# A decoder layer on one core: where three merged activation quads live, and how early weight pairs are begun at a stage border

## The chip, the cores and the metric

The kernel runs on one core of one Trainium2 chip. The metric is the device time of one execution in microseconds (us); a change is judged by the median of several executions. Four engines do the work here: TensorE (PE) multiplies matrices and writes to PSUM banks, VectorE (DVE) and ScalarE (ACT) do elementwise work, GpSimd (POOL) mostly issues DMAs here, and SyncE (SP) issues the weight loads. Each engine works through its own instructions in order; between engines there are semaphore waits.

## The reference

One layer on 256 tokens of width 2048, all in float32. The projection goes to three attention branches of eight heads each and to three gates; each branch result is projected, multiplied by its gate and added up; the sum is projected again. A SwiGLU sub-layer with a hidden width of 5632 and a final norm follow.

```python
def hybrid_mixer(h, w_in, b_gate, ..., w_branch, w_out, lambda_init):
    proj = h @ w_in
    qa, ka, va, qb, kb, vb, qc, kc, vc, g = jnp.split(proj, COL_OFFSETS, axis=-1)
    ...
    br = jnp.stack([_merge_heads(o_a), _merge_heads(o_b), _merge_heads(o_c)], axis=2)
    z = jnp.einsum('bsnm,nmd->bsnd', br, w_branch)
    gates = jax.nn.sigmoid((g + b_gate).reshape(b, s, N_BRANCH, D_MODEL))
    merged = jnp.sum(gates * z, axis=2)
    return merged @ w_out

def swiglu(h, w_gate, w_up, w_down):
    return (jax.nn.silu(h @ w_gate) * (h @ w_up)) @ w_down

x = x + hybrid_mixer(rms_norm(x, norm_mix_g), ...)
x = x + swiglu(rms_norm(x, norm_ffn_g), w_ffn_gate, w_ffn_up, w_ffn_down)
return rms_norm(x, final_norm_g)
```

## The kernel before

**Precision.** A float32 operand is split in two float32r parts, high and low, and a product is three matmuls: high by high, high by low, low by high. An activation is kept transposed as a *quad*: a high and a low part of 512 rows by 256 tokens (128 partitions, 4 by 256 each). A weight block of 512 by 512 is loaded whole (one MB, `raw`), and split on the way: ACT copies the high part, DVE subtracts to get the low part (lines 819 and 820 for half a block, `wboth`; lines 805 and 810 for a whole block in the feed-forward, `wh` and `wl`).

**Units and stages.** The work is a list of *units*, each with a `prep` (split a weight) and an `emit` (its matmuls). In the mixing stage a unit is half a raw block on both token halves, 12 matmuls, lines 799 to 801. There are 18 jobs of eight units for q, k and v, with attention run as side work between units. Then for each of four column blocks j come three gate jobs of eight units and three branch jobs of four, and then four output jobs of eight. The feed-forward has eleven jobs of eleven units each, in a form that replaces eight block products by seven (`m_unit`, on combinations `sp` of the activations and sums of weights) for half of the depth, and multiplies the other half plainly (`p_unit`, 24 matmuls). Its matmuls are lines 789, 790 and 793. The down projection ends the list.

**Memory.** There are two pools on the chip. `bigs` has 17 buffers of 8 KB a partition: raw weights, splits, and quads made by `new_both`. `slots` has 15 of 4 KB: everything small, and quads made by `new_quad`, one slot for each part. A tile waits until the last reader of the buffer's previous tile has ended. Stages limit themselves: three raws in the mixing stage and six in the feed-forward (`RAWS`), four parts of prepared splits in the one and nine in the other (`PARTS`).

**Merged quads.** When the third branch of column block j has been added in (`evac_z`, lines 456 and 461), `to_quad` transposes the merged block on PE and writes its quad, ("m", j). The output jobs read the four of them in their order: units 1 and 2 of a job read m(0), units 3 and 4 m(1), and so on.

**Side work.** One step of a queue of generators is taken per unit (`advance(1)`), ahead of that unit's matmuls. After an output job its `go` adds x, transposes it, and writes `ht` (first two jobs) or a quad `hq` (last two, lines 541 and 542). After the second, `combine` makes four sums in two slots (`s12`, `s34`) and seven `sp` tiles, one slot each, one a step. After a feed-forward job, `f_out` transposes its result and stores it by a POOL DMA.

**Order.** Instructions stand on each engine in the order of the program. The main loop prepares ahead and then emits:

```python
    for u, (need, later, stage, _, emit) in enumerate(units):
        prepare_units(u + 4 if stage == "mix" else u + 6)
        advance(1)
        todo, deferred[:] = deferred[:], []
        emit(ready.popleft())
```

`prepare_units` begins units while parts are free. A feed-forward unit is prepared as a pair: `high` when it is begun and `low` a step later, so the two stand at different places in the queues. An `m_unit` adds other raws into its own first (line 611) and then lets POOL add the next weight into a raw by an accumulating DMA (line 621).

Of the kernel before, what the change touches and what calls it, by code (L numbers as in the profile page):

```python
# [27 lines left out]
AF = mybir.ActivationFunctionType  # L28
# [3 lines left out]
P = 128  # L32
# [19 lines left out]
def trunk(ctx, tc, xT, x, gmix, gffn, w_in, b_gate, lq1, lk1, lq2, lk2, subln, w_branch, w_out,  # L52
          w_fg, w_fu, w_fd, gfin, out):
    nc = tc.nc
# [10 lines left out]
    def slot(shape, name, dt=F32):  # L65
        return slots.tile(shape, dt, tag="slot", name=name)

    def big(shape, name, dt=F32):

        return bigs.tile(shape, dt, tag="big", name=name)  # L70
# [78 lines left out]
    def advance(n):  # L149
        while n > 0 and side:  # L150
            try:
                next(side[0])
                n -= 1
            except StopIteration:
                side.popleft()
# [9 lines left out]
    def new_quad(name):  # L165
        return slot([P, 4, S], name + "h", F32R), slot([P, 4, S], name + "l", F32R)

    def new_both():

        t = big([P, 2, 4, S], "hq", F32R)  # L170
        return t[:, 0], t[:, 1]
# [32 lines left out]
    def transposes(dst, srcs):  # L204
        for i, s in enumerate(srcs):
            nc.tensor.transpose(dst[:, i * P:(i + 1) * P], s, ident)  # L206

    def tps():
        return side_ps.tile([P, 512], F32, tag="T", name="tps")
# [4 lines left out]
    def to_parts(ps, h, l):  # L214
        nc.scalar.activation(h, ps, AF.Copy)
        nc.vector.tensor_tensor(l, ps, h.bitcast(F32), OP.subtract)

    def to_quad(key, nat):

        yield  # L220
        h, l = new_both()
        for t in range(2):
            ps = tps()
            transposes(ps, [nat[:, t, i * P:(i + 1) * P] for i in range(4)])
            to_parts(ps.rearrange("p (a b) -> p a b", a=4), h[:, :, t * P:(t + 1) * P],
                     l[:, :, t * P:(t + 1) * P])
            if t == 1:
                quads[key] = (h, l)
            yield
# [222 lines left out]
    def evac_z(n, j):  # L452
        def f(pss):
            s = sig.pop((n, j))
            for t in range(2):
                nc.vector.tensor_tensor(s[:, t], pss[t], s[:, t], OP.mult)  # L456
            if n == 0:
                merged[j] = s
            else:
                m = merged[j]  # L460
                nc.vector.tensor_tensor(m, m, s, OP.add)
                if n == 2:
                    side.append(to_quad(("m", j), m))
        return f
# [101 lines left out]
    f_t = [scratch.tile([P, 4, S], F32, name=f"f_t{j}") for j in range(NCF)]  # L566

    def f_out(j, f):

        yield  # L570
        ft = slot([P, 4, S], "ft")
        for t in range(2):
            ps = tps()
            transposes(ps, [f[:, t, i * P:(i + 1) * P] for i in range(4)])
            nc.scalar.activation(ft[:, :, t * P:(t + 1) * P], ps.rearrange("p (a b) -> p a b", a=4), AF.Copy)
            if t == 1:
                nc.gpsimd.dma_start(f_t[j], ft)
            yield

    f_in = {}  # L580

# [14 lines left out]
    def ffn_job(j):  # L596
# [80 lines left out]
        def up():  # L677

            s = v["s"]
            nc.vector.tensor_tensor(s[:, 1], bank["b6"], s[:, 1], OP.mult)  # L680
            nc.vector.tensor_tensor(v["m1"], bank["b1"], v["m1"], OP.add)
            nc.vector.tensor_tensor(s[:, 0], v["m1"], s[:, 0], OP.mult)
            side.append(f_out(j, s))
# [71 lines left out]
    units = []  # L755
# [175 lines left out]
    at = 0  # L931

    def prepare_units(n):


        nonlocal at, held

        def low_part():
            nonlocal held
            need, gen = begun.popleft()  # L940
            ready.append(next(gen))
            held += need

        while at < len(units) and at < n:
            need, later, stage, prep, _ = units[at]
            room = PARTS[stage] - held
            if len(begun) > 1 and begun[0][0] <= room:
                low_part()
                continue
            if need > room or len(begun) > 1:  # L950
                break
            gen = prep()
            next(gen)
            begun.append((later, gen))
            held += need
            at += 1
            if not later:
                while begun:
                    low_part()
        while begun and (at == len(units) or not ready):  # L960
            low_part()

    prepare_units(3)
    side.append(prepare())
    for u, (need, later, stage, _, emit) in enumerate(units):
        prepare_units(u + 4 if stage == "mix" else u + 6)
        advance(1)
        todo, deferred[:] = deferred[:], []
        emit(ready.popleft())
        held -= need + later  # L970
        for f in todo:
            f()
# [46 lines left out]
```

## Time and profile before

| | |
|---|---|
| median of three executions | 1731.98 us (1722.41 to 1737.12) |
| the profiled execution | 1732.95 us |
| span of its trace | 1730.8 us |
| mean granted PE clock | 0.984 |
| busy: PE, DVE, ACT, POOL | 1675.8, 1065.6, 825.5, 59.4 us |
| HBM read | 343.56 MB |

Lines of a profile name an engine, a source line, an operation and the tiles, written and read; in a timeline the first number is the start from the span's beginning and the second the duration, both in us, and in brackets stands the idle time before, with what ended it. Matmuls are pipelined: a matmul of 128x512 is shown with 0.39 us, while the next one starts after 0.23.

### The profile page before, as it was taken

The numbers are of one execution on the slowest core, as the hardware profiler recorded it, in microseconds if no ns is written. First come the engines' busy times: TensorE is split into PE (matmuls) and PEld (weight loads), VectorE is DVE, ScalarE is ACT, GpSimd is POOL, SyncE is SP. The second block draws the span as 40 slices with busy tenths as digits, with TensorE's granted clock in tenths as the row PEclk, the third lists the DMA queues.
The fourth block names the chain that finished last, engine by engine and source line by source line (L and its number), as shares of the span: only waits on it lengthen the run. The fifth ranks groups of instructions, "written<-read, shape, count | busy, mean of one in ns | idle before, by whom it ended". The sixth has DMA issues, their size and how long they took to land.

```text
span 1730.8 us, 18729 instructions
## 1 busy us (share of the span) xinstructions
PE 1675.8 (97%) x7512; PEld 1369.8 (79%) x7512; DVE 1065.6 (62%) x1077; ACT 825.5 (48%) x950; POOL 59.4 (3%) x87
## 2 busy tenths in 40 slices
PE   9999999999999999986799989999999999999997
PEld 6888888888888887874578868888888888888886
DVE  6676655555655455542155668877778887654563
ACT  7354544444444443432153556655656566443442
POOL 2100000000000000000000000000000001100000
PEclk9999999999999999998799989999999999999999
DMA  9544444454555555542266657888888888755561
GB/s 336 178 170 152 165 169 160 159 176 158 173 204 201 183 194 194 207 153 93 94 219 231 232 157 229 277 270 270 272 261 262 270 268 260 276 176 193 193 238 76
DMA packets 53656, 352.65 MB, mean 204 GB/s; under 512 B 6256, under 2 KB 6528, under 8 KB 13760
## 3 DMA queue, kind: packets, MB, share of 16 engines
q1 hardware_dynamic: 44640, 309.35, 49.4%
q0 software_dynamic: 8208, 41.04, 10.2%
q8 instruction: 59, 0.97, 0.2%
q10 hardware_dynamic: 720, 1.06, 0.2%
q14 instruction: 29, 0.24, 0.0%
HBM read 343.56 MB, written 7.86 MB: 203 GB/s over the span
## 4 chain that ended last, share of the span: by engine, by line
PE 94%; DVE 3%; ACT 2%; DMA 1%; issue 0%; SPq 0%; ACTq 0%
PE acc L800 22%; PE acc L801 22%; PE acc L799 21%; PE acc L789 9%; PE acc L790 8%; PE acc L793 8%; PE tps L206 2%; DVE wboth L820 1%; ACT wboth L819 1%; PE sps L245 1%; DMA raw<-w_in_t 1%; DVE wl L810 1%; DVE raw L611 0%; ACT wh L805 0%; DVE sig L456 0%
## 5 line engine op out<-in xcount | busy, mean ns | idle before, releaser
L820 DVE TENSOR_TENSOR wboth<-raw,wboth 128x1024 fp32r<-128x1024 f32 (+1 forms) x410 | 500.6, 1234 | 379.6 <-ACT wboth L819 379.2
L799 PE MATMUL acc<-wboth,hq 128*128 128x512 f32 x1568 | 632.4, 403 | 17.1 <-ACT wboth L819 17.0
L800 PE MATMUL acc<-wboth,hq 128*128 128x512 f32 x1568 | 620.3, 396 | 12.4 <-DVE wboth L820 12.4
L819 ACT ACTIVATE wboth<-raw 128x1024 fp32r<-128x1024 f32 (+1 forms) x410 | 423.7, 1052 | 413.6 <-PE acc L801 355.9
L801 PE MATMUL acc<-wboth,hq 128*128 128x512 f32 x1568 | 619.6, 395 | 0.0
L799 PEld LDWEIGHTS acc<-wboth,hq 128*128 128x128 f32 x1568 | 299.0, 191 | 86.7 <-ACT wboth L819 25.2
L800 PEld LDWEIGHTS acc<-wboth,hq 128*128 128x128 f32 x1568 | 299.1, 191 | 78.1 <-DVE wboth L820 18.5
L801 PEld LDWEIGHTS acc<-wboth,hq 128*128 128x128 f32 x1568 | 298.7, 190 | 64.2
L810 DVE TENSOR_TENSOR wl<-raw,wh 128x2048 fp32r<-128x2048 f32 x121 | 276.0, 2289 | 81.6 <-PE acc L793 46.5
L805 ACT ACTIVATE wh<-raw 128x2048 fp32r<-128x2048 f32 x121 | 229.0, 1912 | 111.9 <-DVE raw L611 51.0
L789 PE MATMUL acc<-wh,hq 128*128 128x512 f32 x352 | 139.1, 395 | 4.5 <-ACT m L662 4.5
L790 PE MATMUL acc<-wh,hq 128*128 128x512 f32 x352 | 137.9, 392 | 0.0
L789 PE MATMUL acc<-wh,sp 128*128 128x512 f32 x308 | 121.8, 395 | 0.0
L790 PE MATMUL acc<-wh,sp 128*128 128x512 f32 x308 | 120.7, 392 | 0.0
L793 PE MATMUL acc<-wl,hq 128*128 128x512 f32 x352 | 94.5, 390 | 0.0
L793 PE MATMUL acc<-wl,sp 128*128 128x512 f32 x308 | 82.7, 390 | 3.5 <-DVE wl L810 3.5
L789 PEld LDWEIGHTS acc<-wh,hq 128*128 128x128 f32 x352 | 66.6, 189 | 18.5 <-ACT m L662 4.9
L793 PEld LDWEIGHTS acc<-wl,hq 128*128 128x128 f32 x352 | 66.5, 189 | 13.9
L790 PEld LDWEIGHTS acc<-wh,hq 128*128 128x128 f32 x352 | 66.7, 189 | 13.5
L793 PEld LDWEIGHTS acc<-wl,sp 128*128 128x128 f32 x308 | 57.7, 188 | 16.1 <-DVE wl L810 3.9
L789 PEld LDWEIGHTS acc<-wh,sp 128*128 128x128 f32 x308 | 58.4, 190 | 11.8
L790 PEld LDWEIGHTS acc<-wh,sp 128*128 128x128 f32 x308 | 58.3, 189 | 11.9
(185 smaller groups left out, 882.8 us busy)
## 6 DMA issues: line engine op xcount, KB each, us to landing
raw<-w_in_t SPq DMA_DIRECT2D x116, 1024.0 KB, 4.9
raw<-w_fu_t SPq DMA_DIRECT2D x44, 1024.0 KB, 5.0
raw<-w_fg_t SPq DMA_DIRECT2D x44, 1024.0 KB, 6.5
raw<-w_fd_t SPq DMA_DIRECT2D x44, 1024.0 KB, 4.9
raw<-w_branch_t SPq DMA_DIRECT2D x24, 1024.0 KB, 4.9
raw<-w_out_t SPq DMA_DIRECT2D x16, 1024.0 KB, 4.9
raw<-w_fg_t POOLq DMA_DIRECT2D x11, 1024.0 KB, 8.0
raw<-w_fu_t POOLq DMA_DIRECT2D x11, 1024.0 KB, 9.2
```

What stands on the lines that cost most here:

```text
L206: nc.tensor.transpose(dst[:, i * P:(i + 1) * P], s, ident)
L245: nc.tensor.matmul(ps[:, a:b], qt[lo:hi, h, t * P:(t + 1) * P], kt[lo:hi, h, 0:b - a], start=True, stop=True)
L789: nc.tensor.matmul(acc, ah[:, k], wh[:, k], start=first, stop=False, skip_group_check=not start)
L790: nc.tensor.matmul(acc, al[:, k], wh[:, k], start=False, stop=False, skip_group_check=not start)
L793: nc.tensor.matmul(acc, ah[:, k], wl[:, k], start=False, stop=k == 3, skip_group_check=not start)
L799: nc.tensor.matmul(acc, ah[:, k], wh[:, k], start=start and k == 0, stop=False)
L800: nc.tensor.matmul(acc, ah[:, k], wl[:, k], start=False, stop=False)
L801: nc.tensor.matmul(acc, al[:, k], wh[:, k], start=False, stop=stop and k == n - 1)
L805: nc.scalar.activation(h, r, AF.Copy)
L810: nc.vector.tensor_tensor(l, r, h.bitcast(F32), OP.subtract)
L819: nc.scalar.activation(h[:, sl], r[:, sl], AF.Copy)
L820: nc.vector.tensor_tensor(l[:, sl], r[:, sl], h[:, sl].bitcast(F32), OP.subtract)
```

## The change

Three things change. The quads of the first three column blocks are made by `new_quad` (two slots each) rather than `new_both` (one big buffer); the fourth stays. How far ahead a unit may be begun goes by its own stage rather than by the stage of the unit now running: four ahead, and six for a feed-forward unit. And `f_out` makes both of its transpose sets in one step and both copies in the next.

```diff
@@ to_quad
-        h, l = new_both()
+        h, l = new_quad("m") if key[1] < 3 else new_both()
@@ f_out
         yield
+        ps = [tps() for _ in range(2)]
+        for t in range(2):
+            transposes(ps[t], [f[:, t, i * P:(i + 1) * P] for i in range(4)])
+        yield
         ft = slot([P, 4, S], "ft")
         for t in range(2):
-            ps = tps()
-            transposes(ps, [f[:, t, i * P:(i + 1) * P] for i in range(4)])
-            nc.scalar.activation(ft[:, :, t * P:(t + 1) * P], ps.rearrange("p (a b) -> p a b", a=4), AF.Copy)
-            if t == 1:
-                nc.gpsimd.dma_start(f_t[j], ft)
-            yield
+            nc.scalar.activation(ft[:, :, t * P:(t + 1) * P], ps[t].rearrange("p (a b) -> p a b", a=4), AF.Copy)
+        nc.gpsimd.dma_start(f_t[j], ft)
+        yield
@@ prepare_units
-        while at < len(units) and at < n:
+        while at < len(units):
             need, later, stage, prep, _ = units[at]
+            if at >= n + (2 if stage == "ffn" else 0):
+                break
@@ the main loop
-        prepare_units(u + 4 if stage == "mix" else u + 6)
+        prepare_units(u + 4)
```

Up to the border of the two stages every engine keeps its order, and only the buffers differ. Lines behind `f_out` have numbers one higher in the changed kernel (line 820 is 819 before, 821 is 820, 806 is 805, 811 is 810).

On ACT at the end of the fourth output job, from the sixth of the `sp` tiles on, before (the seven `sp` are interleaved with splits, here for that job's units 6 to 8; `wh` are high parts for the feed-forward; the `hq` rows read the transposed x of the third job):

```order
L511 ACTIVATE sp_6609<-s12_6480 128x512
L819 ACTIVATE wboth_6624<-raw_6501 128x1024
L511 ACTIVATE sp_6629<-s34_6481 128x512
L819 ACTIVATE wboth_6644<-raw_6539 128x1024
L819 ACTIVATE wboth_6659<-raw_6539 128x1024
L805 ACTIVATE wh_6676<-raw_6541 128x2048
L805 ACTIVATE wh_6690<-raw_6543 128x2048
L541 ACTIVATE hq_6692<-tps_6693,gf_99 128x256 x2
L805 ACTIVATE wh_6717<-raw_6541 128x2048
L541 ACTIVATE hq_6692<-tps_6719,gf_99 128x256 x2
L805 ACTIVATE wh_6744<-raw_6585 128x2048
```

And now, at the same place:

```order
L511 ACTIVATE sp_6612<-s12_6483 128x512
L820 ACTIVATE wboth_6627<-raw_6504 128x1024
L511 ACTIVATE sp_6632<-s34_6484 128x512
L820 ACTIVATE wboth_6647<-raw_6542 128x1024
L820 ACTIVATE wboth_6662<-raw_6542 128x1024
L806 ACTIVATE wh_6667<-raw_6544 128x2048
L806 ACTIVATE wh_6669<-raw_6546 128x2048
L806 ACTIVATE wh_6686<-raw_6544 128x2048
L806 ACTIVATE wh_6702<-raw_6588 128x2048
L541 ACTIVATE hq_6704<-tps_6705,gf_99 128x256 x2
L806 ACTIVATE wh_6730<-raw_6544 128x2048
L541 ACTIVATE hq_6704<-tps_6732,gf_99 128x256 x2
```

Four high parts stand ahead of the first copies of x where two stood.

On DVE at the same place, before, behind the last split low part of the fourth job (`wl` are low parts, line 611 adds raws, line 522 adds the fourth job's result to x and so frees its banks):

```order
L820 TENSOR_TENSOR wboth_6659<-raw_6539,wboth_6659 128x1024
L542 SCALAR_TENSOR_TENSOR hq_6692<-tps_6693,gf_99,hq_6692 128x256 x2
L810 TENSOR_TENSOR wl_6714<-raw_6541,wh_6676 128x2048
L611 TENSOR_TENSOR raw_6541<-raw_6541,raw_6545 128x2048
L542 SCALAR_TENSOR_TENSOR hq_6692<-tps_6719,gf_99,hq_6692 128x256 x2
L522 TENSOR_TENSOR x2_6590<-acc0_6592,x2_6590 128x512
L522 TENSOR_TENSOR x2_6590<-acc1_6593,x2_6590 128x512
L810 TENSOR_TENSOR wl_6742<-raw_6543,wh_6690 128x2048
```

And now:

```order
L821 TENSOR_TENSOR wboth_6662<-raw_6542,wboth_6662 128x1024
L811 TENSOR_TENSOR wl_6683<-raw_6544,wh_6667 128x2048
L612 TENSOR_TENSOR raw_6544<-raw_6544,raw_6548 128x2048
L811 TENSOR_TENSOR wl_6700<-raw_6546,wh_6669 128x2048
L542 SCALAR_TENSOR_TENSOR hq_6704<-tps_6705,gf_99,hq_6704 128x256 x2
L811 TENSOR_TENSOR wl_6726<-raw_6544,wh_6686 128x2048
L612 TENSOR_TENSOR raw_6544<-raw_6544,raw_6546 128x2048
L542 SCALAR_TENSOR_TENSOR hq_6704<-tps_6732,gf_99,hq_6704 128x256 x2
L522 TENSOR_TENSOR x2_6593<-acc0_6595,x2_6593 128x512
L522 TENSOR_TENSOR x2_6593<-acc1_6596,x2_6593 128x512
```

Ahead of the two additions of line 522 now stand three low parts and two additions of raws, where one of each stood.

On ACT in the second feed-forward job, before (`ft` is the copy of the transposed result, `m` and `u` are copies that free a bank):

```order
L662 ACTIVATE m_7076<-acc_7063 128x512
L805 ACTIVATE wh_7082<-raw_6939 128x2048
L805 ACTIVATE wh_7102<-raw_6869 128x2048
L575 ACTIVATE ft_7108<-tps_7109 128x4x128
L662 ACTIVATE m_7076<-acc_7115 128x512
L805 ACTIVATE wh_7129<-raw_6962 128x2048
L575 ACTIVATE ft_7108<-tps_7135 128x4x128
L805 ACTIVATE wh_7166<-raw_7061 128x2048
L662 ACTIVATE u_7077<-acc_7063 128x512
```

And now:

```order
L663 ACTIVATE m_7079<-acc_7066 128x512
L806 ACTIVATE wh_7085<-raw_6942 128x2048
L806 ACTIVATE wh_7105<-raw_6872 128x2048
L663 ACTIVATE m_7079<-acc_7121 128x512
L806 ACTIVATE wh_7135<-raw_6965 128x2048
L577 ACTIVATE ft_7141<-tps_7111 128x4x128
L577 ACTIVATE ft_7141<-tps_7112 128x4x128
L806 ACTIVATE wh_7169<-raw_7064 128x2048
L663 ACTIVATE u_7080<-acc_7066 128x512
```

Both copies now stand together, behind the second `m` and ahead of the `u`.

## The prediction

> **What bounds the kernel now.** I read the page's slices first, then windows over the thin ones, then PE's waits, then the timeline inside them. A unit is below one weight split of 512 or 256 rows with the matmuls on it (12 of 128x512; a pair of token halves in the feed-forward, "p", has 24).
>
> ```profile
> span 1730.8 us, 18729 instructions
> PE   9999999999999999986799989999999999999997
> PEclk9999999999999999998799989999999999999999
> ```
>
> PE is full except in slices 18 to 20 and in slice 24. The windows (us, PE busy and count, PEld, DVE, ACT, POOL, clock, DMA share, GB/s) show their size:
>
> ```profile
> 692.00:752.00 60.00, 60.00 (x266) 49.71 (x265) 30.96 (x29) 25.43 (x25) 0.08 (x1) 1.00 0.58 202
> 752.00:872.00 120.00, 88.08 (x275) 62.52 (x275) 35.86 (x35) 26.25 (x26) 0.00 (x0) 0.83 0.28 97
> 872.00:1002.00 130.00, 130.00 (x587) 107.62 (x586) 75.73 (x77) 63.46 (x76) 0.72 (x1) 1.00 0.64 230
> 1002.00:1036.00 34.00, 26.06 (x106) 20.66 (x105) 25.02 (x19) 17.75 (x21) 1.80 (x2) 0.85 0.65 168
> 1036.00:1100.00 64.00, 64.00 (x289) 53.02 (x288) 52.99 (x42) 40.76 (x35) 3.17 (x4) 1.00 0.76 248
> ```
>
> Count matmuls, not busy time: 752 to 872 has 275 in 120 us, the stretch before it 266 in 60. PE's waits are few and all there:
>
> ```profile
> PE acc L799 <- ACT wboth L819: 17.0, 15, 1.1
> PE acc L800 <- DVE wboth L820: 12.4, 19, 0.8
> PE tps L206 <- DVE sig L461: 7.2, 2, 5.0
> ```
>
> One unit of the thin stretch, from the timeline (start, duration, engine, line):
>
> ```profile
> 831.24 0.40 PE L801 MATMUL acc<-wboth,hq 128*128 128x512 f32 x1
> 831.67 1.06 ACT L819 ACTIVATE wboth<-raw 128x1024 fp32r<-128x1024 f32 x1 [5.73 <-PE acc L801]
> 832.76 1.23 DVE L820 TENSOR_TENSOR wboth<-raw,wboth 128x1024 fp32r<-128x1024 f32 x1 [5.57 <-ACT wboth L819]
> 832.78 0.51 PE L799 MATMUL acc<-wboth,hq 128*128 128x512 f32 x1 [1.15 <-ACT wboth L819]
> 834.04 0.77 PE L800 MATMUL acc<-wboth,hq 128*128 128x512 f32 x1 [0.76 <-DVE wboth L820]
> 834.61 0.63 PE L801 MATMUL acc<-wboth,hq 128*128 128x512 f32 x1
> 838.46 1.06 ACT L819 ACTIVATE wboth<-raw 128x1024 fp32r<-128x1024 f32 x1 [5.73 <-PE acc L801]
> ```
>
> ACT may write the next split only when PE has read the last one: a single split buffer, strictly serial, 838.46 - 831.67 = 6.79 us a unit. That follows from the code. Of 17 big buffers four hold h, six the branch outputs, three the raw weights; the merged quads m(0), m(1), m(2) take one each as column blocks are finished, so four buffers for splits become three, two and, from the last block's gates on, one.
>
> **Term 1, the merged quads in slots.** m(0) to m(2) leave the big pool, so all gates keep four split buffers. What the full rate is worth there:
>
> ```profile
> 664.49 0.63 PE L206 MATMUL tps<-ident,sig 128*128 128x128 f32 x4 [2.24 <-DVE sig L461]
> 769.16 1.04 PE L206 MATMUL tps<-ident,sig 128*128 128x128 f32 x4 [4.96 <-DVE sig L461]
> 1002.87 0.60 PE L206 MATMUL tps<-ident,x 128*128 128x128 f32 x4
> 1003.23 0.48 PE L799 MATMUL acc<-wboth,hq 128*128 128x512 f32 x1
> 1037.98 0.91 PE acc L793 x4
> 1040.70 0.91 PE acc L793 x4
> ```
>
> A unit at full rate takes 1040.70 - 1037.98 = 2.72 us (the last two rows, from the chain), a group of four transposes 1003.23 - 1002.87 = 0.36. The group at 769.16 (m(2)) stands ahead of the last block's second unit, the one at 1002.87 ahead of the seventh unit of the fourth output job: 35 + 24 + 6 = 65 units and 8 groups, 65 x 2.72 + 8 x 0.36 = 179.7 us. They took 233.7: 54.0 lost. The waits ahead of the m(2) and m(1) groups (4.96, 2.24) are the same shortage: the merging L456/L461 stand on DVE behind a split low part that waits for a buffer; ahead of m(0)'s group, with four buffers, there is no such wait. Sum 61.2. Bounds: with two buffers 692 to 752 ran at full rate, so four should lose nothing; were half of the 54.0 kept by something else, the term would be 34.2. I take 61.2. Raw weights are no limit by the rows: one MB in 5.44 us is 193 GB/s, and 202 flowed at 692.
>
> **Term 2, the border to the feed-forward.** Here both the slots and the earlier start act, against each other. The durations and the old waits:
>
> ```profile
> 985.00 0.61 ACT L511 ACTIVATE sp<-s 128x512 fp32r<-128x512 f32 x1
> 987.36 1.22 DVE L820 TENSOR_TENSOR wboth<-raw,wboth 128x1024 fp32r<-128x1024 f32 x1
> 988.49 0.69 DVE L512 TENSOR_TENSOR sp<-s,sp 128x512 fp32r<-128x512 f32 x1
> 1003.51 0.48 ACT L541 ACTIVATE hq<-tps,gf 128x256 fp32r<-128x256 f32 x1 [4.88 <-PE tps L206]
> 1004.02 0.48 DVE L542 SCALAR_TENSOR_TENSOR hq<-tps,gf,hq 128x256 fp32r<-128x256 f32 x1 [9.10 <-ACT hq L541]
> 1005.44 2.28 DVE L810 TENSOR_TENSOR wl<-raw,wh 128x2048 fp32r<-128x2048 f32 x1
> 1007.76 2.29 DVE L611 TENSOR_TENSOR raw<-raw 128x2048 f32<-128x2048 f32 x1
> 1010.15 1.92 ACT L805 ACTIVATE wh<-raw 128x2048 fp32r<-128x2048 f32 x1 [5.14 <-DVE raw L611]
> 1013.89 1.28 DVE L522 TENSOR_TENSOR x<-acc,x 128x512 f32<-128x512 f32 x2
> 1017.41 1.28 PE L793 MATMUL acc<-wl,sp 128*128 128x512 f32 x4 [3.46 <-DVE wl L810]
> 1021.88 0.40 PE L789 MATMUL acc<-wh,sp 128*128 128x512 f32 x1
> 1026.59 0.88 POOL L621 DMA_DIRECT2D raw<-w_fu_t  x1 [14.97 <-DVE wl L810]
> 1030.47 0.59 ACT L662 ACTIVATE m<-acc 128x512 f32<-128x512 f32 x1
> 1031.12 0.80 PE L789 MATMUL acc<-wh,hq 128*128 128x512 f32 x1 [4.49 <-ACT m L662]
> 1035.99 0.40 PE L789 MATMUL acc<-wh,sp 128*128 128x512 f32 x1
> ```
>
> Call the fourth output job's units o1 to o8 and the feed-forward's f1 to f5 (m0, m2, m4, p, m5). From the transposes ahead of o7 (1002.87) to f5 (1035.99) went 33.1 us; full rate is 7 x 2.72 + 4 x 0.36 = 20.5. So 12.6 are lost: DVE's low part for f2 is late (3.46), then ACT's copy of a bank for f4 (4.49), the rest is slow clock (1017.41 to 1021.88 after the first, and again after the second).
>
> Now slots: at the combining step 15 must hold 6 halves of m, 3 blocks of x, 2 ht, 2 sums: 13. The first two sp fit, the third takes a freed ht, the fourth and fifth must wait for m(0)'s halves, read last by o2, the last two for m(1)'s, read last by o4. These waits stand on ACT ahead of the splits for o4 and after. Counted from T0, the end of o2 (1002.87 - 4 x 2.72 = 991.99 in this trace): sp on ACT 0.2 to 0.8, the split for o4 to 1.75; DVE has sp 0.69, two L522 1.28, then o4's low part, done at 3.9. PE wants it at 2.95: 1.0 lost. The next pair costs 0.15 at o6. ACT ends o8's split at 10.75 (before: it began wh for f1 at T0 + 2.9). Then, in the new order, wh f1, f2 to 14.4; DVE wl f1 14.9, add 17.1, wl f2 19.4; ACT wh f3 19.05, wh f4 20.9; only then the L541/L542 pair (1003.51 to 1005.44, 1.95) to 22.85; wl f3 25.1, second add 27.3; ACT wh f5 29.25; the other pair 31.2; and only then the two L522 of the fourth job, 32.4. PE reaches the transposes of that x, ahead of f3, at 23.6 and needs those L522: a wait of 8.9. Slow clock for 4.5 us as after the 3.46: f3 ends at 37.7, f4's first bank at 40.7, its second waits for ACT's copy to 40.75 and ends at 43.5. Before, f5 began at T0 + 44.0. **Term 2 is -0.5**: the earlier pairs are eaten by the later start of ACT and by L522's place behind three low parts and two additions. POOL's two accumulating loads move with the additions and low parts ahead of them; the second, issued behind f5's low part, goes out at T0 + 36.9 where it went at 34.6 (1026.59), and its raw is next split for f10, which starts past T0 + 60. SP's loads keep their order. Bounds: nothing lost at all, -12.6; three more handoffs of the sort at 1003.51, +6.
>
> The Trainium skill, "TensorE: Matmul & The Clock Gate", section "HAM oscillation — how this bites in real kernels", holds that only gaps over some 3.4 us bring the clock down. By it the 1.0 at o4 costs only itself. The trace differs: gaps of 1.15 and 0.76 at 832 are followed by matmuls of 0.63, and from 834.04 eleven at full rate would have ended 1.7 earlier. By that row o4 would cost 1.7 more; but the transposes at 664.49, after 2.24 idle, are followed by full rate, which is nearer (one gap, not a train), so I add nothing.
>
> **Term 3, f_out.** Same eight transposes and two copies a job, both copies now behind m5's bank copy and ahead of u2's.
>
> ```profile
> ACT u L662 <- PE acc L793: 41.7, 22, 4.0
> ```
>
> ACT waits 41.7/22 = 1.9 us for PE ahead of such a copy, one more 0.6 copy fits; PE is full from 1036 on, so there is nothing to gain either. Zero, covered by that slack; without the cover 11 x 0.6 = 6.6. The store of f is issued in the same unit as before. In the down stage the new limit of four is the one that its four parts set already: zero.
>
> **Sum.** The profiled execution took 1732.95 (2.15 around its span); less 61.2, less 0.5: 1671.2. The median shown is 0.97 lower: **1670**.
>
> **Rivals.** *The border runs clean* (18 in 100): ACT's 4.88 and DVE's 9.10 of waiting before 1004 are filled, and L522 comes in time. Then 12 more go: 1658. Against: L522's place in DVE's order. *Half of term 1 stays* (14 in 100), because raw weights or evacuations bind once splits do not: 1732 - 34 = 1698, or 1685 if a quarter stays. Against: 202 GB/s at full PE in 692 to 752. *Slower* (2 in 100): in each of eleven feed-forward jobs u2's bank copy, now behind both copies of f, is late for m6, as m5's was at 1031.12. A wait of 4.49 and its slow clock (some 2.1) are 6.6, eleven times 72.6: 1743. It decides from 61.7/11 = 5.6 us a job; the slack of 1.9 speaks against. *The change does not act* (2 in 100): the slots' waits serialize what the big pool did; but from T0 to f5 there are only 11 units, at 4.07 lost each 45 us: 1716 at most with term 1 intact, 1732 only if raws also bind.
>
> **Numbers.** Forecast, 64 in 100: 1662 to 1677 (the two terms right to a few us, and a median of runs that lay from 1722.41 to 1737.12). The range reaches to the clean border and a quarter of term 1: 1658 to 1683. A measurement here can tell about 1% from no change: faster by more 0.95, within 0.03, slower 0.02.
>
> **What would show it.** 752 to 810 in the new trace at 266 matmuls per 60 us, no ACT wait on L801 followed by a PE wait on the split; the transposes ahead of f3 waiting about 9 us for L522; a PE wait near 1 us on the low part of o4. Wrong, if PE waits in the gates for raw weights, if the border's wait is under 3 or over 14, or if PE shows gaps once a job after the border.

## The result and the profile after

| | before | changed |
|---|---|---|
| median | 1732.08 us | 1670.86 us |
| lowest to highest, 4 runs each | 1722.41 to 1737.12 | 1670.27 to 1671.43 |
| the profiled execution | 1732.95 us | 1671.43 us |
| span of its trace | 1730.8 us | 1669.3 us |
| mean granted PE clock | 0.984 | 0.996 |

The ratio is 0.9653, with a 95% interval of 0.9611 to 0.9695: faster by 3.5%, 61 us, where 1670.0 had been forecast. The page of the changed kernel first, its span and the slices of PE and of PE's clock:

```profile
span 1669.3 us, 18730 instructions
PE   9999999999999999999999899999999999999997
PEclk9999999999999999999999989999999999999999
```

The thin slices 18 to 20 are gone. Slices are now 41.7 us long; the one that is left, number 23, with the clock low in number 24, is the border (930 to 975 us). The windows say it in matmuls (us, PE busy and count, PEld, DVE, ACT, POOL, clock, DMA share, GB/s):

```profile
692.00:752.00 60.00, 60.00 (x266) 49.70 (x265) 32.84 (x32) 25.25 (x24) 0.71 (x1) 1.00 0.55 192
752.00:812.00 60.00, 60.00 (x270) 49.66 (x269) 33.21 (x32) 26.55 (x27) 1.43 (x2) 1.00 0.66 231
812.00:872.00 60.00, 60.00 (x270) 49.68 (x269) 37.93 (x37) 27.60 (x29) 0.00 (x0) 1.00 0.68 240
955.00:975.00 20.00, 12.68 (x47) 10.17 (x48) 15.72 (x15) 13.20 (x17) 0.88 (x1) 0.74 0.69 206
1040.00:1600.00 560.00, 560.00 (x2511) 464.34 (x2510) 396.10 (x264) 304.25 (x257) 26.66 (x39) 1.00 0.76 248
```

From 752 to 872 there were 275 matmuls in 120 us; now there are 538 (two of the 270 and 270 stand in both windows). DMA carries 231 to 240 GB/s there where it carried 97. From 1040 to 1600 PE has no gap. PE's longest waits (us in total, times, longest):

```profile
PE tps L206 <- DVE x L522: 7.8, 1, 7.8
PE acc L801 <- DVE wboth L821: 1.8, 4, 0.8
PE wps L86 <- DVE ones L81: 1.3, 1, 1.3
PE acc L800 <- ACT wboth L820: 0.6, 2, 0.4
```

The waits for splits (17.0 and 12.4) and for the merging (7.2) have become 2.4 in all. At the border a single new wait of 7.8 stands where there were two, of 3.5 and 4.5. (The wait of 1.3 lies at the start of the execution, in both kernels.) The timeline of the changed kernel there, with the two merging groups ahead of it (start, duration, engine, line; idle time before and its releaser in brackets):

```profile
662.00 0.60 PE L206 MATMUL tps<-ident,sig 128*128 128x128 f32 x4
760.88 0.60 PE L206 MATMUL tps<-ident,sig 128*128 128x128 f32 x4
930.58 0.63 ACT L511 ACTIVATE sp<-ht 128x512 fp32r<-128x512 f32 x1 [12.63 <-PE acc L801]
934.32 0.50 PE L801 MATMUL acc<-wboth,mh 128*128 128x512 f32 x1 [0.61 <-DVE wboth L821]
934.66 0.40 PE L802 MATMUL acc<-wboth,ml 128*128 128x512 f32 x1
936.92 0.63 ACT L511 ACTIVATE sp<-s 128x512 fp32r<-128x512 f32 x1 [3.29 <-PE acc L801]
940.82 3.71 ACT L806 ACTIVATE wh<-raw 128x2048 fp32r<-128x2048 f32 x2
942.45 0.60 PE L206 MATMUL tps<-ident,x 128*128 128x128 f32 x4
961.46 1.28 DVE L522 TENSOR_TENSOR x<-acc,x 128x512 f32<-128x512 f32 x2
962.20 1.50 PE L206 MATMUL tps<-ident,x 128*128 128x128 f32 x4 [7.76 <-DVE x L522]
963.92 0.63 PE L791 MATMUL acc<-wh,sp 128*128 128x512 f32 x1
968.50 0.60 PE L206 MATMUL tps<-ident,x 128*128 128x128 f32 x4
970.14 0.59 ACT L663 ACTIVATE m<-acc 128x512 f32<-128x512 f32 x1
974.44 0.39 PE L790 MATMUL acc<-wh,sp 128*128 128x512 f32 x1
```

The two rows of ACT's L511 are the waits for slots: 930.58 is the moment at which o2 ends (T0, 930.6), and 936.92 that at which o4 ends. Everything that ACT does for the feed-forward stands behind them; its first `wh` begins at 940.82, T0 + 10.2. The row at 962.20 is the new wait of PE ahead of f3, and 974.44 is the start of f5.

So the 61.5 us between the two spans split as follows. The m(1) group comes at 662.00 instead of 664.49, and the m(2) group at 760.88 instead of 769.16: 8.3 us by then. From the m(2) group to o7's transposes it takes 942.45 - 760.88 = 181.6 instead of 1002.87 - 769.16 = 233.7: 52.1. From there to f5 974.44 - 942.45 = 32.0 instead of 33.1: 1.1. The sum is 61.5.

### The profile page after: what moved, and what is told of

Read it like the earlier page. It is cut to its first block, busy times and chain, and to the rows that moved or that the text cites. A ratio compares the mean times of both kernels' runs of the same rounds, so it can differ in the third digit from the quotient of the medians.

```text
span 1669.3 us, 18730 instructions
## 1 busy us (share of the span) xinstructions
PE 1648.2 (99%) x7512; PEld 1357.8 (81%) x7512; DVE 1065.6 (64%) x1077; ACT 824.3 (49%) x950; POOL 60.0 (4%) x87
## 4 chain that ended last, share of the span: by engine, by line
PE 97%; DVE 1%; ACT 1%; DMA 1%; issue 0%; SPq 0%; ACTq 0%; DVEq 0%
PE acc L800 22%; PE acc L802 22%; PE acc L801 22%; PE acc L790 9%; PE acc L791 9%; PE acc L794 9%; PE tps L206 2%; PE sps L245 1%; DMA raw<-w_in_t 1%; ACT wh L806 0%; DVE raw L612 0%; DVE wl L811 0%; ACT wboth L820 0%; PE sps L258 0%; PE sps L259 0%
## 5 line engine op out<-in xcount | busy, mean ns | idle before, releaser
L800 PE MATMUL acc<-wboth,hq 128*128 128x512 f32 x1472 | 586.5, 398 | 0.7 <-ACT wboth L820 0.6
L801 PE MATMUL acc<-wboth,hq 128*128 128x512 f32 x1472 | 573.4, 390 | 1.2 <-DVE wboth L821 1.2
L802 PE MATMUL acc<-wboth,hq 128*128 128x512 f32 x1472 | 574.5, 390 | 0.0
L802 PEld LDWEIGHTS acc<-wboth,hq 128*128 128x128 f32 x1472 | 276.2, 188 | 59.7
L800 PEld LDWEIGHTS acc<-wboth,hq 128*128 128x128 f32 x1472 | 276.5, 188 | 58.8 <-issue 2.7
L801 PEld LDWEIGHTS acc<-wboth,hq 128*128 128x128 f32 x1472 | 276.8, 188 | 57.3 <-DVE wboth L821 2.5
L794 PEld LDWEIGHTS acc<-wl,sp 128*128 128x128 f32 x308 | 58.4, 190 | 12.4
```

The source lines that it names most:

```text
L794: nc.tensor.matmul(acc, ah[:, k], wl[:, k], start=False, stop=k == 3, skip_group_check=not start)
L800: nc.tensor.matmul(acc, ah[:, k], wh[:, k], start=start and k == 0, stop=False)
L801: nc.tensor.matmul(acc, ah[:, k], wl[:, k], start=False, stop=False)
L802: nc.tensor.matmul(acc, al[:, k], wh[:, k], start=False, stop=stop and k == n - 1)
```

## The experiments

One theory stood behind all of them: nearly all of the gain is the four split buffers in the gates; at the border the early start of the feed-forward pairs is worth several us, but the seven `sp`, which now wait on ACT for slots, give them back. Its rivals were that the earlier start alone matters at the border, that the order of DVE (L522 behind three low parts) is what costs there, and that `f_out` counts. Runs of one batch share the runs of the kernel before: the first four have 1731.89 us (13 runs, 1724.49 to 1737.85), the last three 1733.85 (6 runs, 1724.12 to 1737.80).

The measure for the border is the stretch from the transposes ahead of o7 to the first matmul of f5, 33.1 us before and 32.0 in the changed kernel; at full rate it would be 20.5. The wait at o4 lies ahead of it.

### The slots alone

```diff
 (kernel before)
-        h, l = new_both()
+        h, l = new_quad("m") if key[1] < 3 else new_both()
```

> The kernel before with the first three merged quads in slots, nothing else. By the theory of the prediction term 1 comes whole and the border keeps the old order but gets the slots' waits: DVE has the first hq pair ahead of the first low part, f2's low part comes about 5 us late and f4's second bank again waits for ACT's copy; f5 begins about 46 us after the end of o2 (43.8 in the changed kernel), so 1673 us. Rival, that the earlier pairs carry a large part of the gain: over 1680.

Measured: 1674.20 us (1673.37 to 1674.87), ratio 0.9654 (0.9635 to 0.9673). From the timeline of this run, o7's transposes, the two waits of PE and f5:

```profile
943.01 0.60 PE L206 MATMUL tps<-ident,x 128*128 128x128 f32 x4
958.89 2.07 PE L793 MATMUL acc<-wl,sp 128*128 128x512 f32 x4 [4.80 <-DVE wl L810]
972.65 0.79 PE L789 MATMUL acc<-wh,hq 128*128 128x512 f32 x1 [4.65 <-ACT m L662]
976.99 0.39 PE L789 MATMUL acc<-wh,sp 128*128 128x512 f32 x1
```

The line of `to_quad` alone brings 57.7 of the 61 us. The stretch from o7 to f5 is 976.99 - 943.01 = 34.0, with the two waits of before still there (3.46 has become 4.80, 4.49 is 4.65). That is 0.9 more than before, and about 1.0 is lost at o4 besides, where the trace shows an idle time of 0.61: at the border the slots cost about 2 us.

### The border alone

```diff
 (kernel before)
-        while at < len(units) and at < n:
+        while at < len(units):
             need, later, stage, prep, _ = units[at]
+            if at >= n + (2 if stage == "ffn" else 0):
+                break
...
-        prepare_units(u + 4 if stage == "mix" else u + 6)
+        prepare_units(u + 4)
```

> The kernel before with the earlier pairs alone: merged quads in the big pool, f_out as it was. By the theory the gates keep their 59 us of loss, and the border, without the slots' waits, starts its high parts at once: the transposes ahead of f3 wait about 2 us for line 522, f5 begins about 36 us after the end of o2 rather than 44, so 8 us less than before, about 1724. Rival, that the order on DVE and not the slots is what holds the border: f5 at 42 or later, 1730.

Measured: 1727.86 us (1714.54 to 1730.92, 10 runs), ratio 0.9964 (0.9940 to 0.9988). From its timeline:

```profile
997.73 3.72 ACT L805 ACTIVATE wh<-raw 128x2048 fp32r<-128x2048 f32 x2 [1.66 <-PE acc L801]
1005.22 3.72 ACT L805 ACTIVATE wh<-raw 128x2048 fp32r<-128x2048 f32 x2 [3.77 <-DVE raw L611]
1005.69 0.60 PE L206 MATMUL tps<-ident,x 128*128 128x128 f32 x4
1019.95 0.33 PE L206 MATMUL tps<-ident,x 128*128 128x128 f32 x1 [2.27 <-DVE x L522]
1031.41 0.39 PE L789 MATMUL acc<-wh,sp 128*128 128x512 f32 x1
```

The stretch is 1031.41 - 1005.69 = 25.7: the early start by itself is worth 33.1 - 25.7 = 7.4 us. ACT's first `wh` begins 8.0 us ahead of o7's transposes (997.73 to 1005.69), as it did in the kernel before; in the changed kernel it begins 1.6 ahead of them (940.82 to 942.45). What the early start moves is the third `wh`: it begins 0.5 ahead of these transposes (1005.22), where before it began 7.3 behind them (1010.15 and 1002.87). The whole execution gained 4.0 by the medians, where 8 had been expected. The profiled one came to o7 2.8 us later than the profiled execution before (1005.69 and 1002.87). These 2.8 us lie in the thin stretch, which this kernel still has (from the m(2) group to o7 it took 236.8 instead of 233.7); the interval of the ratio, 2.1 to 10.4 us, holds both.

With the slots present, the same edit is worth 34.0 - 32.0 = 2.0 in this stretch. So the two parts do not add up at the border.

### `f_out` as before

```diff
 (changed kernel)
-        ps = [tps() for _ in range(2)]
-        for t in range(2):
-            transposes(ps[t], [f[:, t, i * P:(i + 1) * P] for i in range(4)])
-        yield
         ft = slot([P, 4, S], "ft")
         for t in range(2):
+            ps = tps()
+            transposes(ps, [f[:, t, i * P:(i + 1) * P] for i in range(4)])
...
```

> The changed kernel with f_out as before. By the theory the copies lie in ACT's slack and PE is full in the feed-forward: 1670.9, within 1 us of the changed kernel. Rival, that moving the copies is worth something in each of eleven jobs: 3 to 7 us more.

Measured: 1671.36 us (1670.60 to 1671.51), 0.5 from the changed kernel's 1670.86, with ranges that overlap. The edit of `f_out` is worth nothing that can be measured.

### Two quads in the slots

```diff
 (changed kernel)
-        h, l = new_quad("m") if key[1] < 3 else new_both()
+        h, l = new_quad("m") if key[1] < 2 else new_both()
```

> The changed kernel with only m(0) and m(1) in slots. The gates of the last block then have three split buffers rather than four, still at full rate by the theory; the first five sp fit without a wait and the last two wait only for o2. ACT ends o8's split about 5 us earlier, line 522 too, the wait ahead of f3 falls from 7.8 to about 4.5, f5 begins about 38 us after o2: 1665. Rival, that the big buffer is missed in the last gates: a loss there of several us and 1671 or more; rival, that the slots' waits do not set the border: 1671.

Measured: 1663.51 us (1663.34 to 1664.04), ratio 0.9592 (0.9570 to 0.9615), 7.9 below the run with `f_out` undone of the same batch. From its timeline:

```profile
930.88 0.63 ACT L511 ACTIVATE sp<-s 128x512 fp32r<-128x512 f32 x1 [10.25 <-PE acc L801]
934.78 3.70 ACT L806 ACTIVATE wh<-raw 128x2048 fp32r<-128x2048 f32 x2
941.79 0.60 PE L206 MATMUL tps<-ident,x 128*128 128x128 f32 x4
955.45 1.28 DVE L522 TENSOR_TENSOR x<-acc,x 128x512 f32<-128x512 f32 x2
956.19 0.33 PE L206 MATMUL tps<-ident,x 128*128 128x128 f32 x1 [2.41 <-DVE x L522]
957.78 0.63 PE L791 MATMUL acc<-wh,sp 128*128 128x512 f32 x1
967.64 0.39 PE L790 MATMUL acc<-wh,sp 128*128 128x512 f32 x1
```

This is the run that settles the border. With two slots more, no `sp` waits for the end of o4: the wait of 3.29 is gone, and `wh` begins at 934.78 instead of 940.82, 6.0 earlier. DVE's order is as in the changed kernel, with the three low parts still ahead of L522, and the chain from that `wh` to L522 is as long as there: 955.45 - 934.78 = 20.7, and 961.46 - 940.82 = 20.6. L522 comes 6.0 earlier, PE waits 2.41 and 0.27 ahead of f3 instead of 7.76, and the stretch is 967.64 - 941.79 = 25.9, that of the border alone. The expectation had left 4.5 of waiting there; it was right on the slots and too careful on their price. The big buffer costs nothing in the gates: from the m(2) group (761.17) to o7 it takes 180.6, the changed kernel's 181.6 less the 1.0 at o4, so three split buffers keep them full. This version is faster than both kernels.

### One quad in the slots

```diff
 (changed kernel)
-        h, l = new_quad("m") if key[1] < 3 else new_both()
+        h, l = new_quad("m") if key[1] < 1 else new_both()
```

> The changed kernel with only the quad of m0 in the small slots; those of m1 and m2 lie in the split buffers, as m3 to m5 do. Theory (a wait for a small slot on ScalarE holds what stands behind it): no split of the border waits for a slot, so the border is as with two quads there, f5 at about T0+36.6, 0.5 us or less from it; but the gates of the last two output jobs have split buffers less by one more, and the merging of m1 then waits again as in the kernel before, about 2.2 us there. 1666 us, between 1664 and 1668. Rival (each quad taken out of the slots shortens the border further): under 1661. Rival (any buffer taken from the gates brings back part of the waits of the 65 units): above 1672.

Measured: 1666.55 us (1665.40 to 1667.42), ratio 0.9622 (0.9572 to 0.9672). From its timeline:

```profile
762.59 0.66 PE L206 MATMUL tps<-ident,sig 128*128 128x128 f32 x4 [2.24 <-DVE sig L461]
763.48 0.63 PE L801 MATMUL acc<-wboth,hq 128*128 128x512 f32 x1
766.46 0.40 PE L802 MATMUL acc<-wboth,hq 128*128 128x512 f32 x1
944.82 0.60 PE L206 MATMUL tps<-ident,x 128*128 128x128 f32 x4
970.52 0.39 PE L790 MATMUL acc<-wh,sp 128*128 128x512 f32 x1
```

The stretch at the border is 25.7, no shorter than with two quads. What is lost is a merging wait of 2.24, the size forecast from m(1)'s in the kernel before. The expectation named the wrong quad (there are four, m(0) to m(3), and the gates concerned are those of the last two column blocks): the wait stands ahead of m(2)'s group (762.59; 760.88 in the changed kernel), which now meets the two split buffers that m(1) met before. From 812 to 872 PE has 271 matmuls in 60 us, a full stretch. So two split buffers are enough for the gates' units, and one too few for the merging.

### Five ahead instead of six, with three quads and with two

```diff
 (changed kernel; the second run has also key[1] < 2)
-            if at >= n + (2 if stage == "ffn" else 0):
+            if at >= n + (1 if stage == "ffn" else 0):
```

> The changed kernel (three quads in the slots) with the pairs of the border begun at most five units ahead instead of six. One theory: the long wait ahead of f3 comes from VectorE doing the low part of a later pair before the addition of f1's result (L522); begun a unit later, it stands behind, and the wait falls from 7.8 us to 3 or less; that alone gives 1665 to 1666. The other: the wait is only where the chain behind the slots shows, which is ScalarE held by slot waits and then its splits in a row; then L522 comes earlier, the wait ahead of f3 falls, but f4 waits 5 to 6 us for a copy of ScalarE, f5 begins at about T0+43.2 as before, and the time is 1669 to 1671.

> Two quads in the slots and the pairs of the border begun at most five units ahead. By the first theory of the run with three quads and five ahead (the order of VectorE is what costs), this gains on the version with two quads and six ahead, 1661 to 1662.5; by the other (ScalarE held by the slots is what costs, and with two quads nothing of it is left), it is the same within 1 us, 1663 to 1664.5, or worse, since each split comes a unit later.

Measured: 1670.88 us (1670.69 to 1671.36) with three quads, 1664.15 (1662.60 to 1664.69) with two. The timeline of the run with three:

```profile
940.60 3.71 ACT L806 ACTIVATE wh<-raw 128x2048 fp32r<-128x2048 f32 x2
942.22 0.60 PE L206 MATMUL tps<-ident,x 128*128 128x128 f32 x4
955.35 0.33 PE L206 MATMUL tps<-ident,x 128*128 128x128 f32 x1 [0.82 <-DVE x L522]
960.51 1.92 ACT L806 ACTIVATE wh<-raw 128x2048 fp32r<-128x2048 f32 x1 [6.33 <-DVE raw L612]
962.68 1.19 PE L794 MATMUL acc<-wl,hq 128*128 128x512 f32 x4 [1.05 <-DVE wl L811]
969.65 0.79 PE L790 MATMUL acc<-wh,hq 128*128 128x512 f32 x1 [5.79 <-ACT m L663]
974.23 0.39 PE L790 MATMUL acc<-wh,sp 128*128 128x512 f32 x1
```

And of the run with two:

```profile
941.69 0.60 PE L206 MATMUL tps<-ident,x 128*128 128x128 f32 x4
963.70 0.50 PE L790 MATMUL acc<-wh,hq 128*128 128x512 f32 x1 [3.63 <-ACT m L663]
968.13 0.39 PE L790 MATMUL acc<-wh,sp 128*128 128x512 f32 x1
```

With three quads L522 now comes in front of the third low part and the second addition of raws, and the wait that the trace had shown as the longest falls from 7.76 to 0.82 and 0.27. The stretch stays at 974.23 - 942.22 = 32.0: PE waits 5.79 for ACT's copy of a bank for f4 instead. That copy stands on ACT behind the `wh` of 960.51, which waited 6.33 for the addition that L522 was moved ahead of. Whoever had gone by the table of waits would have mended the order of DVE and gained nothing: splits and additions form one chain through ACT and DVE, it begins with ACT's first `wh` (940.60, late by the slots as in the changed kernel), and a new order only changes which of its links PE meets last. With two quads the stretch is 26.4, and five ahead gives nothing either.

| version | o7 to f5 | wait at o4 | median |
|---|---|---|---|
| before | 33.1 | none | 1731.9 |
| slots alone | 34.0 | 0.61 | 1674.2 |
| border alone | 25.7 | none | 1727.9 |
| changed: both, three quads | 32.0 | 0.61 | 1670.9 |
| the same, `f_out` as before | 32.0 | 0.61 | 1671.4 |
| five ahead, three quads | 32.0 | 0.61 | 1670.9 |
| two quads | 25.9 | none | 1663.5 |
| five ahead, two quads | 26.4 | none | 1664.2 |
| one quad | 25.7 | none | 1666.6 |

## Why the prediction was right

**Term 1 (-61.2).** The 65 units and 8 groups took 181.6 us, of which 1.0 is lost at o4 and belongs to the border: o7's transposes came 942.45 - 930.6 = 11.85 after T0 instead of 10.88. That leaves 180.6 where 179.7 had been worked out, and 53.1 saved instead of 54.0. The merging waits and their aftermath gave 8.3 instead of 7.2. Together 61.4. The bounds were not touched: raw weights flowed at 231 to 240 GB/s and held nobody up. The step that carried it was to count matmuls in a stretch in which PE looked three quarters busy, and to read the 6.79 us of a unit as one buffer's round.

**Term 2 (-0.5).** Measured from T0 = 930.6, f5 began at T0 + 43.8, where 43.5 had been worked out and 44.0 was the old value: -0.2. The steps in between, forecast and measured:

| step, after T0 | forecast | measured |
|---|---|---|
| lost at o4 (idle time 0.61 in the trace) | 1.0 | 1.0 |
| `wh` of f1 begins on ACT | 10.75 | 10.2 |
| L522 done on DVE | 32.4 | 32.1 |
| PE's wait ahead of f3 | 8.9 | 7.76 |
| end of f3 | 37.7 | 37.9 |
| ACT's copy for f4 done | 40.75 | 40.1 |
| f5 begins | 43.5 | 43.8 |

The wait ahead of f3 was forecast 1.1 too long: the first transposition needs only the first of the two L522, which ends 0.64 earlier, L522 itself was 0.3 early, and PE came 0.2 late. The phase of half rate that follows (matmuls shown with 0.63 and started every 0.43, instead of 0.39 and 0.23) was forecast too short: it lasted through nearly all of f3, whose transposes and matmuls took 968.50 - 962.20 = 6.3 us where 5.3 had been allowed. ACT's copy for f4 was ready before PE asked for it. That these errors cancelled was luck; the order of the steps, and the one that PE waits long for, were not.

Adding nothing for the clock at o4 was right: behind the wait of 0.61 the first matmul is shown with 0.50, the next (934.66) with 0.40, and so are the following ones.

The forecast that the two parts of the change act against each other at the border is shown by the pair of runs with one part alone (34.0 and 25.7, and 32.0 with both), and that the slots' waits on ACT do it by the run with two quads, where taking away one of the two waits brings 6.0 us at ACT's first `wh`, 6.0 at L522 and 6.1 in the stretch. One point of the prediction was put too evenly: it has the earlier pairs "eaten by the later start of ACT and by L522's place behind three low parts and two additions". With five ahead L522's place changes and nothing is gained, with three quads or with two; with the slots freed and the order kept, nearly all of the loss is gone. So the later start of ACT is enough to explain it, and L522's place only decides where it shows.

**Term 3 (0).** The run with `f_out` undone agrees within 0.5 us, and from 1040 to 1600 PE has no gap. From f5 to the end of the trace both kernels take the same 694.8 to 694.9 us, so the new limit in the down stage counts for nothing either, as forecast. The slack that was to cover the moved copy is there still:

```profile
ACT u L663 <- PE acc L794: 40.6, 22, 4.0
```

That is 40.6/22 = 1.8 us a copy, 1.9 before.

**The rivals.** Half of term 1 left: no, with 266 to 270 matmuls per 60 us throughout the gates. The change does not act: no. Slower by u2's copy: no. A clean border, 1658: not here, but the version with two quads, 7 us below, goes more than half of the way; what it still loses against full rate, 25.9 - 20.5 = 5.4 us, is the 2.41 and 0.27 ahead of f3 and the half rate after them.

## What to carry to other kernels

Where an engine seems three quarters busy, count its instructions against a full stretch, and look for one buffer that two engines hand back and forth; here the three buffers freed for it were worth 57.7 us, and the reordering at the border 7.4 at most. But a buffer moved between pools makes new waits where the other pool is used, and such a wait stands in order on an engine: everything behind it starts late, and the trace shows the loss far from it, under another name. Before mending the longest wait in the table, ask what would end last without it, and move as few buffers as fill the thin stretch: two quads here, not three.

## What the hardware showed unexpectedly

The length of an idle stretch does not by itself say whether the matmuls after it run at half rate. In the kernel before, 2.24 us ahead of the group at 664.49 are followed by full rate (665.18, matmuls of 0.39 and 0.40). In the run with one quad the same 2.24 ahead of the group at 762.59 are followed by matmuls of 0.63 until 766.46. After 2.41 and 0.27 in the run with two quads, half rate comes at once (957.78); after 2.27 and 0.27 in the run with one quad, only with the fifth matmul (960.99). The Trainium skill, "TensorE: Matmul & The Clock Gate", section "HAM oscillation — how this bites in real kernels", puts the bound at idle gaps of more than some 3.4 us; the gap of 7.76 agrees, and so does the 2.24 of the kernel before, but the 2.24 with one quad and the 2.41 with two do not, so that here the measurement decides. What tells the two gaps of 2.24 apart was not tried and stays open.

The kernel before varied by 15 us from run to run (1722.41 to 1737.12), and so did the version with the border alone (1714.54 to 1730.92), the two that keep the thin stretch. Of the versions without it none varied by more than 2.1 us. In the kernel before and in the border alone, longer runs had a lower mean granted clock (0.982 at 1730.92, 0.991 at 1714.54), as if the half-rate phases in each unit of that stretch came now more, now less often; no run here shows what decides it.
